# The last stage of an encoder block: h2 kept in the output tensor, half of the residual added by accumulating transfers, y handled in pairs of tiles

## The chip, the cores and the metric

One core of one Trainium2 chip runs the whole program. The metric is the device time of one launch in microseconds (us), the median of several runs. The profile is one execution taken by the hardware profiler. Its engines are PE (TensorE, matrix multiplication), DVE (VectorE), ACT (ScalarE), POOL (GpSimd) and SP (SyncE, which here only issues transfers). Each engine works through its own instructions in their fixed order and waits at an instruction until the data for it are there.

## What is computed

512 tokens of width 2048 pass through one layer: a mixing block with attention and a convolution, and then a gated feed-forward block. Only the end matters here:

```python
u = rms_norm(h, ffn_pre_g[l])            # h is called h2 below
gate, up = jnp.split(u @ w_gate_up[l], 2, axis=-1)
f = (jax.nn.silu(gate) * up) @ w_down[l] # f is called y below
h = h + rms_norm(f, ffn_post_g[l])
```

`rms_norm(x, g)` is x times 1/sqrt(mean(x*x) + 1e-6) times g, with the mean over the 2048 features of a token. So y must be complete for a token before its scale is known, and the residual h2 is added last.

## The kernel before

All activations are stored transposed: 128 features of a tile lie on the 128 partitions, and the tokens lie along the free dimension. y has 16 tiles of 128 features by 512 tokens. A is the first half of the tokens (256), B the second half.

h2 is made in the middle of the program (line 907): 16 stores of 128x512 put it into a scratch tensor in device memory, `h_d`. The product with `w_down` is cut along its 44 row tiles. Most of it is done earlier and summed up in a scratch tensor `y_d`. The last four row tiles (`DN_3`) are left for the end, which works so:

1. `half(0)` handles tokens A, `half(1)` tokens B. Each runs over 8 pairs of tiles, o = 0, 2, ..., 14. For a pair, `four` (line 1066) issues 24 matmuls of 128x256 into one PSUM bank, `pl`: 12 for each of the two tiles. Line 1199 adds the part of `y_d` to each tile, on DVE. Line 1202 squares each tile on ACT into `ysq`. Line 1210 sums the squares of the pairs on DVE. In the second half, line 1206 also writes y times the gain g into `yg`, on ACT.
2. The squares of the last two tiles are not added on DVE. Line 1212 folds the sum from 512 to 256 columns, and TensorE adds all of it over the partitions (line 357, `r_s`), three products of which the last waits for the last square.
3. `rstd` makes 1/rms: DVE scales and adds the epsilon (line 365, `r_v`), POOL raises it to the power -1/2 (line 367, `r_r`), and TensorE spreads the result over all partitions (line 374, `r_b`).
4. For tokens A, `finish` multiplies each of 16 tiles by g and `r_b` (line 1242, DVE), adds h2 (line 1248, three of four on POOL, one on DVE) and stores it (line 1249, SP's queue). h2 comes from `h_d` in the tiles `ha`. 12 of the 16 tiles are put between the work of the second half by a priority, and the last 4 are done after the last sum of squares.
5. For tokens B, `yg` is held in four groups of four tiles. After the last `r_b`, line 1260 multiplies each group by it. Group 0 is added into the output by an accumulating transfer, over a copy of h2 that was stored there before. For groups 1 to 3, line 1266 adds h2 from the tiles `hb` in two parts on DVE, and line 1271 stores each part, in turn on SP's and ACT's queues.

TensorE's order matters: `r_s` and `r_b` of tokens A (called `r40_s` and `r40_b`) stand among the matmuls of the second half, in the order that the program's scheduler gives, as far as the program does not pin it (`keep_in_program_order`).

Of the kernel before, what the change touches and what calls it, by code (L numbers as in the profile page):

```python
# [74 lines left out]
def hybrid_block(ctx: ExitStack, tc, xT, vecs, rpb, mask, w_c0, w_qk, w_v, w_gg, w_cg, w_ao, w_co, w_out, w_g0, w_gu, w_dn, outT):  # L75
# [1084 lines left out]
    for o in range(KT):  # L1160
        if o == KT - 2:
            added()
        tc.keep_in_program_order(nc.gpsimd.dma_start(y[o][:, A], y_d[0, o, :, A]))
    ha = []

    def second_loads(o):

        if o == KT - AHEAD:
            for i in range(KT):
                load_in_order(y[i][:, B], y_d[0, i, :, B])  # L1170
        elif o == KT - AHEAD + 2:
            for i in range(0, KT - 4, 4):
                t = stp.tile([P, 4, HN], F32, tag="S" if i else "S1", name=f"ha{i}")
                load_in_order(t, h_d[i : i + 4, :, A].rearrange("k p t -> p k t"))
                ha.extend(t[:, m] for m in range(4))
            for i in range(KT - 4, KT, 2):
                t = stp.tile([P, 2, HN], F32, tag="quad", name=f"ha{i}", bufs=3)
                load_in_order(t, h_d[i : i + 2, :, A].rearrange("k p t -> p k t"))
                ha.extend((t[:, 0], t[:, 1]))

    yg, r4 = [], []

    def half(n, between={}):

        cols, other = ((A, B), (B, A))[n]
        acc, last = None, []
        for o in range(0, KT, 2):
            if n == 0 and o + AHEAD < KT:
                kept(o + AHEAD)
# [6 lines left out]
            sq = [slot(f"ysq{n}_{o}")] * 2 if o < KT - 2 else [slot(f"ysq{n}_{o + i}") for i in range(2)]  # L1196
            for i, part in enumerate((other, cols)):
                t = y[o + i][:, cols]
                add = nc.vector.tensor_tensor(out=t, in0=ps[:, part], in1=t, op=ALU.add)
                if n == 0:  # L1200
                    tc.keep_in_program_order(add)
                nc.scalar.activation(sq[i][:, part if o < KT - 2 else cols], t, AF.Square)
                if n:
                    if (o + i) % 4 == 0:
                        yg.append(wp.tile([P, 4, HN], F32, tag="raw", name=f"yg{o}", bufs=5))
                    nc.scalar.activation(yg[-1][:, (o + i) % 4], t, AF.Copy, scale=col(C_FPOST, o + i))
            if o == 0:
                acc = sq[0]
            elif o < KT - 2:
                nc.vector.tensor_tensor(out=acc, in0=acc, in1=sq[0], op=ALU.add)  # L1210
# [14 lines left out]
    hb = []

    def first_half():
        s2()
        for i in range(0, KT, 4):
# [1 line left out]
            load_in_order(hb[-1], h_d[i : i + 4, :, B].rearrange("k p t -> p k t"))
        for g in range(G_ADD):

            nc.sync.dma_start(ov[4 * g : 4 * g + 4, :, B].rearrange("k p t -> p k t"), hb[g])
        with tc.high_priority(offset=-TAIL):
            finish(range(KT - LEFT), False)

    def finish(ms, pin):

        for m in ms:  # L1240
            ym = y[m][:, A]
            ins = nc.vector.scalar_tensor_tensor(  # L1242
                out=ym, in0=ym, scalar=col(C_FPOST, m), in1=r4[-1][:, A], op0=ALU.mult, op1=ALU.mult
            )
            if pin:
                tc.keep_in_program_order(ins)
            e = nc.vector if m % 4 == 3 else nc.gpsimd
            e.tensor_tensor(out=ym, in0=ym, in1=ha[m], op=ALU.add)  # L1248
            nc.sync.dma_start(ov[m, :, A], ym)
# [7 lines left out]
    for g, t in enumerate(yg):

        out = hb[g] if g < G_ADD else t
        tc.keep_in_program_order(nc.vector.tensor_tensor(out=out, in0=t, in1=rb, op=ALU.mult))  # L1260
        if g < G_ADD:
            nc.gpsimd.dma_start(ov[4 * g : 4 * g + 4, :, B].rearrange("k p t -> p k t"), out, accum_op=ALU.add)
            continue
        for m in range(0, 4, 2):
            tc.keep_in_program_order(
                nc.vector.tensor_tensor(  # L1266
                    out=t[:, m : m + 2], in0=t[:, m : m + 2], in1=hb[g][:, m : m + 2], op=ALU.add
                )
            )
            q = nc.scalar if m else nc.sync  # L1270
            q.dma_start(ov[4 * g + m : 4 * g + m + 2, :, B].rearrange("k p t -> p k t"), t[:, m : m + 2])
# [86 lines left out]
```

## Time and profile before

| what | us |
|---|---|
| median of 3 runs | 2492.33 (2490.29 to 2495.18) |
| span of the profiled execution, first to last instruction | 2489.2 |
| median less span | 3.1 |
| PE busy | 2464.8 (99%) |
| DVE busy | 2073.3 (83%) |
| ACT busy | 1246.1 (50%) |
| POOL busy | 493.3 (20%) |

The profiled execution has no time of its own in the profile apart from its span. A row of the timeline gives start, duration, engine, line, operation, output and inputs, shapes, and in brackets how long the engine had stood idle and what ended that. Start plus duration of one instruction can lie after the start of the next, since instructions of one engine overlap a little at their ends. SPq and ACTq are the queues that issue transfers.

### The profile page before, as it was taken

What the parts mean: (1) busy time and instruction counts of PE and PEld (TensorE: products, weight loads), DVE (VectorE), ACT (ScalarE), POOL (GpSimd) and SP (SyncE); (2) the same over time, 40 slices, a digit from 0 to 9 for tenths busy, and PEclk for the clock granted to TensorE, in tenths of its full rate; (3) what the DMA queues carried; (4) which work ended last, traced back from release to release, by engine and by line L of the source; (5) the groups of instructions that cost most, each with busy time, mean ns of one, the idle gap of its engine ahead of it and who ended that gap; (6) DMA issues with size and microseconds to landing.
All of it is one profiled execution on the core that took longest, in us unless ns stands there. A gap on an engine that the chain in (4) does not pass through costs nothing. (4 is left out here: it accounts for less than half of the span.)

```text
span 2489.2 us, 36170 instructions
## 1 busy us (share of the span) xinstructions
PE 2464.8 (99%) x13495; PEld 2141.7 (86%) x13495; DVE 2073.3 (83%) x2743; ACT 1246.1 (50%) x1939; POOL 493.3 (20%) x583
## 2 busy tenths in 40 slices
PE   9999999999999999999999999999999999999997
PEld 8888888888888888889998888888888888888887
DVE  5999887497777668878898888889898889989887
ACT  5223333355555434556455555555555565456553
POOL 0110242220000000021111111122222203632352
PEclk9999999999999999999999999999999999999998
DMA  6246222376667544669456655666666678888986
GB/s 215 89 144 207 101 103 101 135 253 196 190 187 228 184 142 136 205 215 301 138 166 178 185 170 171 184 195 213 205 200 195 220 234 238 237 230 255 226 222 195
DMA packets 165104, 472.37 MB, mean 190 GB/s; under 512 B 18752, under 2 KB 30656, under 8 KB 164928
## 3 DMA queue, kind: packets, MB, share of 16 engines
q1 hardware_dynamic: 109584, 334.02, 39.1%
q0 software_dynamic: 32928, 97.54, 18.4%
q10 hardware_dynamic: 22416, 38.50, 4.1%
q8 instruction: 106, 1.74, 0.3%
q14 instruction: 70, 0.57, 0.1%
HBM read 396.06 MB, written 71.30 MB: 188 GB/s over the span
## 5 line engine op out<-in xcount | busy, mean ns | idle before, releaser
L450 DVE SCALAR_TENSOR_TENSOR cv<-z,vec,cv 128x497 f32<-128x497 f32 (+14 forms) x240 | 188.4, 786 | 4.8
L971 POOL TENSOR_TENSOR row<-row,asq 128x512 f32<-128x512 f32 x30 | 54.6, 1821 | 402.8 <-ACT asq L970 402.8
L1126 POOL TENSOR_TENSOR ys<-ys,row 128x512 f32<-128x512 f32 x32 | 57.6, 1801 | 119.8 <-DVE ys L347 100.1
L146 ACT CAST whi_qk<-raw_qk 128x1024 fp32r<-128x1024 f32 x32 | 33.7, 1053 | 79.2 <-PE qk L196 58.2
L147 DVE TENSOR_TENSOR wlo_qk<-raw_qk,whi_qk 128x1024 fp32r<-128x1024 f32 x32 | 40.4, 1262 | 37.9 <-ACT whi_qk L146 37.8
L993 POOL TENSOR_TENSOR an<-an,row 128x512 f32<-128x512 f32 x32 | 55.3, 1729 | 72.1 <-DMA an<-a_d 45.7
L146 ACT CAST whi_y<-raw_y 128x1024 fp32r<-128x1024 f32 x31 | 32.6, 1051 | 64.9 <-PE py L196 52.7
L760 DVE TENSOR_TENSOR gg<-py,gg 128x512 f32<-128x512 f32 x32 | 21.9, 687 | 46.4 <-PE py L197 43.4
L531 POOL TENSOR_TENSOR bm<-braw,msk 128x64 f32<-128x64 f32 x96 | 54.3, 600 | 14.8 <-DMA braw<-in_rpb 14.7
L193 PE MATMUL py<-ycl,whi_y 128*128 128x512 f32 x128 | 49.9, 390 | 0.0
L196 PE MATMUL py<-ych,whi_y 128*128 128x512 f32 x128 | 49.8, 389 | 0.0
L197 PE MATMUL py<-ych,wlo_y 128*128 128x512 f32 x128 | 49.8, 389 | 0.0
L147 DVE TENSOR_TENSOR wlo_y<-raw_y,whi_y 128x1024 fp32r<-128x1024 f32 x31 | 37.8, 1224 | 9.0 <-ACT whi_y L146 8.6
L458 POOL TENSOR_TENSOR csum<-csum,cv 128x512 f32<-128x512 f32 x7 | 12.7, 1816 | 141.4 <-DVE cv L450 141.4
L177 PE MATMUL f<-b,wlo_f 128*128 128x256 f32 x128 | 36.3, 283 | 0.0
L176 PE MATMUL f<-b,whi_f 128*128 128x256 f32 x128 | 36.3, 283 | 0.0
L175 PE MATMUL f<-b,whi_f 128*128 128x256 f32 x128 | 36.3, 283 | 0.0
L146 ACT CAST whi_ca<-raw_ca 128x1024 fp32r<-128x1024 f32 x12 | 12.6, 1054 | 46.3 <-PE cb L196 18.1
L787 POOL DMA_DIRECT2D m_d<-m x8 | 4.4, 555 | 136.9 <-ACT m L169 75.0
L568 ACT ACTIVATE sc<-sc,st 128x256 f32<-128x256 f32 x32 | 16.1, 504 | 30.8 <-DVE st L567 30.8
L1127 POOL DMA_DIRECT2D y_d<-ys x32 | 29.4, 918 | 9.4 <-POOL ys L1126 7.8
L1056 DVE TENSOR_TENSOR sg<-sg,su 128x512 f32<-128x512 f32 x39 | 30.0, 770 | 0.0
(3251 smaller groups left out, 8755.6 us busy)
## 6 DMA issues: line engine op xcount, KB each, us to landing
raw_qk<-in_w_qk SPq DMA_DIRECT2D x32, 512.0 KB, 3.3
raw_w<-in_w_dn SPq DMA_DIRECT2D x24, 512.0 KB, 5.4
a_d<-sg ACTq DMA_DIRECT2D x44, 256.0 KB, 4.0
raw_v<-in_w_v SPq DMA_DIRECT2D x16, 512.0 KB, 4.3
gg<-g_d SPq DMA_DIRECT2D x32, 256.0 KB, 4.1
raw_y<-in_w_co SPq DMA_DIRECT2D x16, 512.0 KB, 3.6
raw_f<-in_w_g SPq DMA_DIRECT2D x16, 512.0 KB, 3.9
an<-a_d POOLq DMA_DIRECT2D x32, 256.0 KB, 5.5
```

What stands on the lines that cost most here:

```text
L146: cast(hi[:, s], raw[:, s])
L147: nc.vector.tensor_tensor(out=lo[:, s], in0=raw[:, s], in1=hi[:, s].bitcast(F32), op=ALU.subtract)
L175: nc.tensor.matmul(o, hi, t[:, B], start=first, stop=False, skip_group_check=True)
L176: nc.tensor.matmul(o, hi, t[:, A], start=False, stop=False, skip_group_check=True)
L193: mmul = nc.tensor.matmul(ps, hi[:, s], al, start=first, stop=False)
L196: nc.tensor.matmul(ps, hi[:, s], ah, start=False, stop=False)
L197: nc.tensor.matmul(ps, lo[:, s], ah, start=False, stop=last)
L450: nc.vector.scalar_tensor_tensor(out=a[:, to], in0=z[:, fr], scalar=col(C_WDW, i * CW + w), in1=a[:, to], op0=ALU.mult, op1=ALU.add)
L531: nc.gpsimd.tensor_tensor(out=bm[:, o + i - i0], in0=raw[:, :, min(max(i, 0), 3) * EC : (min(max(i, 0), 3) + 1) * EC], in1=msk[:, o + i - ...
L971: nc.gpsimd.tensor_tensor(out=row[n], in0=row[n], in1=sq, op=ALU.add)
L993: ins = nc.gpsimd.dma_start(t, a_d[DN_P + k]), nc.gpsimd.tensor_tensor(out=t, in0=t, in1=row[k // KT], op=ALU.mult)
L1126: tc.keep_in_program_order(nc.gpsimd.tensor_tensor(out=t, in0=t, in1=row[n], op=ALU.mult))
```

## The change

- `h_d` is gone. h2 is stored into the output tensor instead, with the same 16 stores on ACT's queue.
- y is held in tiles of a pair for one half of the tokens (128x2x256), so each pair is loaded by one transfer instead of two, and the add and the square of a pair are one instruction of 128x512 each. The last pair still has two of each.
- The gain g is now multiplied in on ACT in both halves, in place for tokens A.
- 1/rms is made by a square root on ACT (with 1/2048 and the epsilon in the same instruction) and a reciprocal on DVE.
- Tokens A: DVE multiplies a pair by `r_b` (8 instructions of 128x512), and an accumulating transfer on POOL's queue adds it into the output, where h2 already lies. The loads `ha`, the 16 adds and the 16 stores are gone, and so is the priority: the 8 multiplications stand where the program writes them.
- Tokens B: group 0 is added by an accumulating transfer as before, now without a copy of h2 first. The four multiplications come first, then the adds: the first parts of groups 1 and 2 on POOL, the other four parts on DVE.

The core of the diff:

```diff
-                nc.scalar.dma_start(h_d[i], f[i])
+                nc.scalar.dma_start(ov[i], f[i])
...
+    def weighted(n, o):
+        t = y[n][o // 2][:, o % 2]
+        return nc.scalar.activation(yg[-1][:, o % 4] if n else t, t, AF.Copy, scale=col(C_FPOST, o))
...
-            for i, part in enumerate((other, cols)):
-                t = y[o + i][:, cols]
-                add = nc.vector.tensor_tensor(out=t, in0=ps[:, part], in1=t, op=ALU.add)
-                nc.scalar.activation(sq[i][:, part if o < KT - 2 else cols], t, AF.Square)
+            if o < KT - 2:
+                tc.keep_in_program_order(nc.vector.tensor_tensor(out=t, in0=halves, in1=t, op=ALU.add))
+                sq = slot(f"ysq{n}_{o}")
+                nc.scalar.activation(sq.rearrange("p (m t) -> p m t", m=2), t, AF.Square)
+                if o:
+                    nc.vector.tensor_tensor(out=acc, in0=acc, in1=sq, op=ALU.add)
...
-            lambda: r.append(rstd(squares, D, f"r4{n}", blocks, pin)),
+            nc.scalar.activation(r, ps[:, : NB // 2], AF.Sqrt, bias=eps, scale=1.0 / D)
+            nc.vector.reciprocal(r, r)
...
-        with tc.high_priority(offset=-TAIL):
-            finish(range(KT - LEFT), False)
+        ra = r4[0][:, None].broadcast_to([P, 2, HN])
+        for o in range(0, KT, 2):
+            t = y[0][o // 2]
+            nc.vector.tensor_tensor(out=t, in0=t, in1=ra, op=ALU.mult)
+            nc.gpsimd.dma_start(ov[o : o + 2, :, A].rearrange("k p t -> p k t"), t, accum_op=ALU.add)
...
-    finish(range(KT - LEFT, KT), True)
+    tc.keep_in_program_order(weighted(1, KT - 1))
     last2()
...
+    scale_group(0)
+    tc.keep_in_program_order(
+        nc.gpsimd.dma_start(ov[:4, :, B].rearrange("k p t -> p k t"), yg[0], accum_op=ALU.add)
+    )
+    scale_group(1)
+    add_part(nc.gpsimd, nc.sync, 1, 0)
+    scale_group(2)
+    add_part(nc.gpsimd, nc.sync, 2, 0)
+    scale_group(3)
+    for n, (g, m) in enumerate(((1, 2), (2, 2), (3, 0), (3, 2))):
+        add_part(nc.vector, (nc.scalar, nc.sync)[n % 2], g, m)
```

The new order follows from the code and from the scheduler, which places again what is not pinned. Three places matter. Names carry the half and the pair: `pl1_12` is the PSUM bank of pair 12 in the second half (tokens B), `y4b` is pair 4 of tokens B, `r40` belongs to tokens A and `r41` to tokens B. The line numbers after the change are not those of before.

TensorE, where the 1/rms of tokens A is spread, before:

```order
L1066 MATMUL pl1_4_23586<-fa43h_23105,wl5h_23135 128x256
L1066 MATMUL pl1_4_23586<-fa43h_23105,wl5l_23136 128x256
L374 MATMUL r40_b_23611<-ident_77,r40_r_23576 128x128 x2
L1066 MATMUL pl1_6_23668<-fa40l_23094,wl6h_23187 128x256
L1066 MATMUL pl1_6_23668<-fa40h_23093,wl6h_23187 128x256
```

The same place of TensorE after the change:

```order
L1063 MATMUL pl1_12_23709<-fa43l_23105,wl13h_23306 128x256
L1063 MATMUL pl1_12_23709<-fa43h_23104,wl13h_23306 128x256
L1063 MATMUL pl1_12_23709<-fa43h_23104,wl13l_23307 128x256
L372 MATMUL r40_b_23583<-ident_77,r40_23486 128x128 x2
L1063 MATMUL pl1_6_23615<-fa40l_23093,wl6h_23180 128x256
L1063 MATMUL pl1_6_23615<-fa40h_23092,wl6h_23180 128x256
```

Before, `r40_b` stood behind the pairs 0, 2 and 4 of the second half. Now it stands behind the pairs 0, 2, 4, 8 and 12, and the pairs 6, 10 and 14 come after it.

DVE in the second half, before:

```order
L1199 TENSOR_TENSOR y4_23153<-pl1_4_23586,y4_23153 128x256
L1199 TENSOR_TENSOR y5_23154<-pl1_4_23586,y5_23154 128x256
L1242 SCALAR_TENSOR_TENSOR y0_23149<-y0_23149,vec_75,r40_b_23611 128x256
L1242 SCALAR_TENSOR_TENSOR y1_23150<-y1_23150,vec_75,r40_b_23611 128x256
L1210 TENSOR_TENSOR ysq1_0_23534<-ysq1_0_23534,ysq1_4_23659 128x512
L1242 SCALAR_TENSOR_TENSOR y2_23151<-y2_23151,vec_75,r40_b_23611 128x256
L1242 SCALAR_TENSOR_TENSOR y3_23152<-y3_23152,vec_75,r40_b_23611 128x256
L1242 SCALAR_TENSOR_TENSOR y4_23153<-y4_23153,vec_75,r40_b_23611 128x256
L1199 TENSOR_TENSOR y6_23155<-pl1_6_23668,y6_23155 128x256
```

DVE at that place after the change:

```order
L1194 TENSOR_TENSOR y2b_23157<-pl1_2_23518,y2b_23157 128x512
L1253 TENSOR_TENSOR y0a_23148<-y0a_23148,r40_b_23583 128x512
L1253 TENSOR_TENSOR y2a_23149<-y2a_23149,r40_b_23583 128x512
L1198 TENSOR_TENSOR ysq1_0_23514<-ysq1_0_23514,ysq1_2_23553 128x512
L1253 TENSOR_TENSOR y4a_23150<-y4a_23150,r40_b_23583 128x512
L1253 TENSOR_TENSOR y6a_23151<-y6a_23151,r40_b_23583 128x512
L1253 TENSOR_TENSOR y8a_23152<-y8a_23152,r40_b_23583 128x512
L1253 TENSOR_TENSOR y10a_23153<-y10a_23153,r40_b_23583 128x512
L1253 TENSOR_TENSOR y12a_23154<-y12a_23154,r40_b_23583 128x512
L1253 TENSOR_TENSOR y14a_23155<-y14a_23155,r40_b_23583 128x512
L1194 TENSOR_TENSOR y4b_23158<-pl1_4_23558,y4b_23158 128x512
L1198 TENSOR_TENSOR ysq1_0_23514<-ysq1_0_23514,ysq1_4_23610 128x512
```

Before, the multiplications of tokens A were spread between the adds of tokens B. Now all eight stand in one block ahead of the add of pair 4, and the add and the sum of squares of the pairs 4, 6, 8, 10 and 12 follow one after the other.

DVE at the end, before (the first row is the last of the adds of y):

```order
L1199 TENSOR_TENSOR y15_23164<-pl1_14_23803,y15_23164 128x256
L365 TENSOR_SCALAR r41_v_23843<-r41_s_23836 128x2
L1242 SCALAR_TENSOR_TENSOR y12_23161<-y12_23161,vec_75,r40_b_23611 128x256
L1242 SCALAR_TENSOR_TENSOR y13_23162<-y13_23162,vec_75,r40_b_23611 128x256
L1242 SCALAR_TENSOR_TENSOR y14_23163<-y14_23163,vec_75,r40_b_23611 128x256
L1242 SCALAR_TENSOR_TENSOR y15_23164<-y15_23164,vec_75,r40_b_23611 128x256
L1248 TENSOR_TENSOR y15_23164<-y15_23164,ha14_23444 128x256
L1260 TENSOR_TENSOR hb0_23614<-yg0_23537,r41_b_23859 128x1024
L1260 TENSOR_TENSOR yg4_23662<-yg4_23662,r41_b_23859 128x1024
L1266 TENSOR_TENSOR yg4_23662<-yg4_23662,hb4_23616 128x512 x2
```

DVE at the end after the change:

```order
L1205 TENSOR_TENSOR y14b_23163<-pl1_14_23742,y14b_23163 128x256 x2
L1238 RECIPROCAL r41_23774<-r41_23774 128x2
L1264 TENSOR_TENSOR yg0_23512<-yg0_23512,r41_b_23785 128x1024
L1264 TENSOR_TENSOR yg4_23608<-yg4_23608,r41_b_23785 128x1024
L1264 TENSOR_TENSOR yg8_23671<-yg8_23671,r41_b_23785 128x1024
L1264 TENSOR_TENSOR yg12_23734<-yg12_23734,r41_b_23785 128x1024
L1268 TENSOR_TENSOR yg4_23608<-yg4_23608,hb4_23586 128x512
L1268 TENSOR_TENSOR yg8_23671<-yg8_23671,hb8_23588 128x512
L1268 TENSOR_TENSOR yg12_23734<-yg12_23734,hb12_23590 128x512 x2
```

The four multiplications and the add that belong to tokens A have left the end. Of the six adds of tokens B, four are left on DVE, behind all multiplications.

More of the change, by code (lines that the diff above doesn't have):

```diff
@@ L66 @@
 AHEAD = 6
-LEFT, G_ADD = 4, 1
 RE_EARLY = 11
@@ L1156, in hybrid_block, with load_y @@
     pairs(1, *products_and_operands(1, DN_2), DN_3)
-    y = [slot(f"y{o}") for o in range(KT)]
-    for o in range(KT):
+    y = [[slot(f"y{o}{n}", shape=(P, 2, HN)) for o in range(0, KT, 2)] for n in "ab"]
+    def load_y(q, n, o):
+        ins = q.dma_start(y[n][o // 2], y_d[0, o : o + 2, :, (A, B)[n]].rearrange("k p t -> p k t"))
+        tc.keep_in_program_order(ins)
+    for o in range(0, KT, 2):
         if o == KT - 2:
             added()
[L1163 to L1181, printed above, removed]
+        load_y(nc.gpsimd, 0, o)
+    yg = []
+    def weighted(n, o):
+        t = y[n][o // 2][:, o % 2]
+        return nc.scalar.activation(yg[-1][:, o % 4] if n else t, t, AF.Copy, scale=col(C_FPOST, o))
     def half(n, between={}):
-        cols, other = ((A, B), (B, A))[n]
-        acc, last = None, []
+        cols = (A, B)[n]
+        acc = None
         for o in range(0, KT, 2):
@@ L1189, in half @@
                 kept(o + AHEAD)
-            elif n == 0:
-                second_loads(o)
+            elif n == 0 and o == KT - AHEAD:
+                for i in range(0, KT, 2):
+                    load_y(nc.sync, 1, i)
             ps = (bank, abank)[o // 2 % 2](f"pl{n}_{o}")
-            for i, part in enumerate((other, cols)):
+            for i, part in enumerate((A, B)):
                 four(ps[:, part], *w[o + i], cols)
             between.get(o, lambda: None)()
-            sq = [slot(f"ysq{n}_{o}")] * 2 if o < KT - 2 else [slot(f"ysq{n}_{o + i}") for i in range(2)]
@@ L1197, in half @@
-            for i, part in enumerate((other, cols)):
-                t = y[o + i][:, cols]
[L1199 to L1210, printed above, removed]
-            if o == KT - 4:
-                nc.vector.tensor_tensor(out=acc[:, cols], in0=acc[:, cols], in1=acc[:, other], op=ALU.add)
-        return acc, *sq
-    def halved(n, squares, pin=False):
-        r = []
-        blocks = range(n * NB // 2, (n + 1) * NB // 2)
-        return (
-            lambda: r.append(rstd(squares, D, f"r4{n}", blocks, pin)),
-            lambda: r4.insert(0, by_column(r[0], f"r4{n}", blocks, pin)),
-        )
+            t = y[n][o // 2]
@@ new lines, in half @@
+            halves = ps.rearrange("p (m t) -> p m t", m=2)
+            if n and o % 4 == 0:
+                yg.append(wp.tile([P, 4, HN], F32, tag="raw", name=f"yg{o}", bufs=5))
+            if o < KT - 2:
[4 more added lines that the diff above has]
+                    nc.vector.tensor_tensor(out=acc, in0=acc, in1=sq, op=ALU.add)
+                else:
+                    acc = sq
+            else:
+                last = []
+                for i in range(2):
+                    tc.keep_in_program_order(
+                        nc.vector.tensor_tensor(out=t[:, i], in0=halves[:, i], in1=t[:, i], op=ALU.add)
+                    )
+                    last.append(slot(f"ysq{n}_{o + i}"))
+                    nc.scalar.activation(last[i][:, A], t[:, i], AF.Square)
@@ new lines, in half, with sums @@
+            if o == KT - 4:
+                tc.keep_in_program_order(
+                    nc.vector.tensor_tensor(out=acc[:, A], in0=acc[:, A], in1=acc[:, B], op=ALU.add)
+                )
+            for i in range(2 - (n and o == KT - 2)):
+                ins = weighted(n, o + i)
+                if o == KT - 2:
+                    tc.keep_in_program_order(ins)
+        return acc, *last
+    eps = const.tile([P, 1], F32, name="eps")
+    nc.gpsimd.memset(eps, EPS)
+    r4 = []
+    def halved(n, squares, pin=False):
+        r = const.tile([P, NB // 2], F32, name=f"r4{n}")
+        def sums():
+            ps = abank(f"r4{n}_s")
+            for i, a in enumerate(squares):
+                for t in range(NB // 2):
+                    mmul = nc.tensor.matmul(
+                        ps[:, t : t + 1], a[:, t * P : (t + 1) * P], ones[:, 0:1],
+                        start=i == t == 0, stop=i == len(squares) - 1, skip_group_check=True,
+                    )
+                    if pin:
+                        tc.keep_in_program_order(mmul)
+            nc.scalar.activation(r, ps[:, : NB // 2], AF.Sqrt, bias=eps, scale=1.0 / D)
+            nc.vector.reciprocal(r, r)
+        return sums, lambda: r4.append(by_column(r, f"r4{n}", range(NB // 2), pin)[:, A])
@@ L1224, in hybrid_block @@
     s1, s2 = halved(0, half(0), pin=True)
[L1225 removed]
+    hb = [None]
     def first_half():
         s2()
[L1229 removed]
+        for i in range(4, KT, 4):
             hb.append(wp.tile([P, 4, HN], F32, tag=("whi", "wlo")[i // 4 % 2], name=f"hb{i}"))
[L1231 to L1236 removed]
@@ L1238, in finish @@
[L1238 to L1249, printed above, removed]
+            load_in_order(hb[-1], ov[i : i + 4, :, B].rearrange("k p t -> p k t"))
@@ L1257, in hybrid_block @@
[L1257 to L1271, printed above, removed]
+    rb = r4[1][:, None].broadcast_to([P, 4, HN])
```

12 lines of the change are left out of this document (9 added, 3 removed).

## The prediction

> **What bounds the kernel now.** I read the page first: engine shares, then the 40 slices.
>
> ```profile
> span 2489.2 us, 36170 instructions
> PE 2464.8 (99%) x13495; PEld 2141.7 (86%) x13495; DVE 2073.3 (83%) x2743; ACT 1246.1 (50%) x1939; POOL 493.3 (20%) x583
> ```
>
> TensorE is busy to the end, and the change leaves its 13,000 matmuls as they are. So only the end, where TensorE runs out of work, can give or take time. The table of windows shows where that is:
>
> ```profile
> 2460.00:2470.00 10.00, 10.00 (x86) 10.00 (x84) 8.92 (x20) 5.49 (x15) 4.10 (x5) 1.00 0.40 133
> 2470.00:2480.00 10.00, 3.25 (x18) 2.50 (x17) 8.32 (x15) 1.66 (x5) 4.32 (x5) 0.71 0.18 62
> ```
>
> The columns are PE, PEld, DVE, ACT and POOL. DVE is busy 8.92 and 8.32 of 10 us there. The chain of waits and the timeline give the steps:
>
> ```profile
> 2469.94 0.28 PE L1066 MATMUL pl<-fa43h,wl15l 128*128 128x256 f32 x1
> 2470.84 0.75 DVE L1199 TENSOR_TENSOR y<-pl,y 128x256 f32<-128x256 f32 x2
> 2472.07 0.40 ACT L1202 ACTIVATE ysq<-y 128x256 f32<-128x256 f32 x1
> 2472.52 0.62 PE r_s L357 x4
> 2473.17 0.16 DVE L365 TENSOR_SCALAR r_v<-r_s 128x2 f32<-128x2 f32 x1 [1.58 <-PE r_s L357]
> 2473.41 0.71 POOL L367 TENSOR_TENSOR r_r<-r_v,mhalf 128x2 f32<-128x2 f32 x1 [6.04 <-DVE r_v L365]
> 2474.17 1.22 PE L374 MATMUL r_b<-ident,r_r 128*128 128x128 f32 x4 [1.04 <-POOL r_r L367]
> 2475.70 1.21 DVE L1260 TENSOR_TENSOR hb<-yg,r_b 128x1024 f32<-128x1024 f32 x1
> 2482.99 1.29 DVE L1266 TENSOR_TENSOR yg<-yg,hb 128x512 f32<-128x512 f32 x2
> 2484.36 0.38 ACTq L1271 DMA_DIRECT2D out<-yg  x1
> ```
>
> So I cut the end in two at 2475.70, where DVE starts on tokens B's output. Ahead of it runs the chain: last matmul, last adds, last square, `r_s`, 1/rms, `r_b`. Behind it lie 13.5 us (2489.2 less 2475.70): DVE's multiplications and adds until 2484.28 (8.6 us), then 4.9 us for the last store.
>
> **The start of the last stretch.** If DVE had nothing else, the change would bring it forward. The four multiplications of tokens A (1.66 us in the chain) and their add stand no longer ahead, the fold no longer delays the last adds, and POOL's 0.71 us is replaced. For the new steps the nearest rows are these:
>
> ```profile
> 1.19 1.28 ACT L119 ACT_TABLE_LOAD   x1 [1.19 <-PEq L1345]
> 2.48 0.20 ACT L119 ACTIVATE mhalf<-ones 128x4 f32<-128x4 f32 x1
> L569 DVE RECIPROCAL st<-st x32: 142/157/166, 299.1 to 485.2; 128x1 f32<-128x1 f32 x32
> ```
>
> The square root of 128x2 costs about 0.20, the reciprocal 0.16, with hand-overs of 0.04 each 0.5 us in all, against 1.0 us from `r_s` to `r_b` before (2473.17 to 2474.17). Table loads stand once in ACT's new order, ahead of the first square root, where ACT waits for `r_s` anyway: nothing if hidden, 1.28 us if not.
>
> But the order of the instructions says that DVE will have something else. `r_b` of tokens A now comes two pairs later on TensorE. The pace:
>
> ```profile
> 2445.25 0.28 PE L1066 MATMUL pl<-fa40l,wl0h 128*128 128x256 f32 x1
> 2451.01 1.40 PE L357 MATMUL r_s<-ones,ysq 128*128 128x1 f32 x12
> 2455.22 0.60 PE L374 MATMUL r_b<-ident,r_r 128*128 128x128 f32 x4
> ```
>
> Two pairs take 2451.01 less 2445.25, so 5.76 us or 2.88 a pair. `r_b` moves from 2455.22 to about 2460.98, and its result is there at 2461.6. In front of DVE's block stands the first multiplication, so DVE waits there with the adds of pairs 4, 8 and 12 behind it, though TensorE has finished those pairs. Behind this wait come 8 multiplications and one sum, then pair after pair an add, a square on ACT, and a sum that waits for the square. This alternation can be measured in the first half of before, where the same three steps followed each other:
>
> ```profile
> 2440.37 0.75 DVE L1199 TENSOR_TENSOR y<-pl,y 128x256 f32<-128x256 f32 x2
> 2440.82 0.75 ACT L1202 ACTIVATE ysq<-y 128x256 f32<-128x256 f32 x2 [1.47 <-DVE y L1199]
> 2441.60 0.69 DVE L1210 TENSOR_TENSOR ysq<-ysq,ysq 128x512 f32<-128x512 f32 x1 [0.48 <-ACT ysq L1202]
> 2442.21 0.75 DVE L1199 TENSOR_TENSOR y<-pl,y 128x256 f32<-128x256 f32 x2
> 2412.60 0.69 DVE L328 TENSOR_TENSOR d<-d,d_14v 128x512 f32<-128x512 f32 x1
> L970 ACT ACTIVATE asq<-sg 128x512 f32<-128x512 f32 x30 | 19.0, 633 | 5.5 <-issue 4.5 <-DVE sg L1056 0.9
> ```
>
> One round took 1.84 us. With pairs as one instruction it is 0.69 (add from PSUM) + 0.03 + 0.63 (square) + 0.04 + 0.61 (from the sum's start to the next instruction) = 2.0 us, since a square can no longer start when the first tile of a pair is ready. The sum:
>
> - 2461.65: first multiplication; 9 instructions of 128x512 at 0.61 end at 2467.1.
> - Five rounds of 2.0 us (pairs 4 to 12): 2477.1. TensorE has been done since 2470.
> - Fold 0.45, two adds 0.76, last square 0.45: 2478.8. `r_s` 0.62 and hand-overs: 2479.45.
> - Square root and reciprocal 0.45, `r_b` 1.22 and hand-overs: 2481.2.
>
> Against 2475.70 that is 5.5 us later. The uncertain pieces are the round (1.84 to 2.1 over five rounds: -0.8 to +0.5) and the first half. There ACT gets two more instructions a pair (0.49 each):
>
> ```profile
> 2427.85 0.74 DVE L1199 TENSOR_TENSOR y<-pl,y 128x256 f32<-128x256 f32 x2
> 2433.92 0.75 DVE L1199 TENSOR_TENSOR y<-pl,y 128x256 f32<-128x256 f32 x2
> 2437.14 0.75 DVE L1199 TENSOR_TENSOR y<-pl,y 128x256 f32<-128x256 f32 x2
> L1206 ACT ACTIVATE yg<-y,vec 128x256 f32<-128x256 f32 x16 | 7.9, 495 | 3.6 <-DVE y L1199 3.6
> ```
>
> The casts of the weights for pairs 8 to 14 go through that queue. A round of 3.2 us there becomes about 3.8. From the first add at 2427.85 on, the weights of pair 14 are then ready at 2443.2, and TensorE, which now has 13 matmuls of the second half mixed in, wants the last of them at about 2444.7. I take nothing; if the cover fails, up to 1 us.
>
> **The last stretch.** Before, DVE had four multiplications (1.13 to 1.21) and six adds (0.61 to 0.69) in it: 8.6 us. Now it has the four (4.6 us) and four adds (2.5 us): 7.1 us if nothing blocks it. What can block it is POOL, which adds two parts beside it:
>
> ```profile
> 2423.43 1.41 POOL L1126 TENSOR_TENSOR ys<-ys,row 128x512 f32<-128x512 f32 x1 [0.19 <-DVE ys L347]
> 2424.04 1.34 DVE L156 TENSOR_TENSOR wl6l<-raw_w,wl6h 128x512 fp32r<-128x512 f32 x1
> 2425.31 2.62 DVE L156 TENSOR_TENSOR wl7l<-raw_w,wl7h 128x512 fp32r<-128x512 f32 x1
> 2425.75 1.63 POOL L1126 TENSOR_TENSOR ys<-ys,row 128x512 f32<-128x512 f32 x1
> 2478.42 1.37 POOL L1262 DMA_DIRECT2D out<-hb  x1 [2.06 <-DVE yg L1260]
> ```
>
> A DVE instruction that took 0.69 elsewhere took 1.34 and 2.62 beside a POOL add, and ended 0.5 us after it. POOL starts on group 0's transfer 2.7 us after DVE's first multiplication began and issues for 1.37, so its two adds (1.3 to 1.8 each) run from about 4.0 to 6.7 us. DVE comes to its adds at 4.6: the first waits until about 5.3, the second until about 6.7, and the fourth ends at 8.6. The gain of 1.5 us is then gone. The Trainium skill, SBUF — State Buffer, Who interferes with whom, says the same as a rule: a VectorE instruction with two SBUF inputs and a GpSimd instruction that reads SBUF exclude each other for the whole instruction. By it the stretch keeps its 8.6 us; by the undisturbed rows it would be 7.1.
>
> Behind the last add come the stores. The traffic stays: one accumulating transfer of 512 KB and six stores of 256 KB.
>
> ```profile
> out<-hb POOLq DMA_DIRECT2D x1, 512.0 KB, 7.0
> 2484.00:2485.00 1.00, 0.00 (x0) 0.00 (x0) 0.28 (x1) 0.00 (x0) 0.00 (x0) 0.50 1.21 245
> 2486.00:2487.00 1.00, 0.00 (x0) 0.00 (x0) 0.00 (x0) 0.00 (x0) 0.00 (x0) 0.50 1.09 384
> ```
>
> The transfers ran at 245 GB/s beside the accumulating one and at 384 without it, at a full share of the DMA engines. In the new order the stores start some 2 us later and closer together, so they catch up no time: 0 to 0.6 us more than 4.9. I take +0.3 and for the whole last stretch 0.0, with -1.5 to +0.8.
>
> **Other edits.** h2's 16 stores have the same size and queue; the loads, adds and stores of tokens A that go away were off the chain apart from the last four tiles, counted above. Eight accumulating transfers of 256 KB now run from about 2463. Group 0's 512 KB took 7.0 us to land, so 2 MB strictly one behind the other take up to 28 us (2491). In the last 15 us of the span its queue showed this:
>
> ```profile
> q0 software_dynamic: 528, 0.52, 25.0%
> ```
>
> 25% of 15 us are 3.75 us of all DMA engines for 0.52 MB, so 15 us for 2 MB if they overlap well. I take the shorter, done near 2479, ahead of group 0's transfer (about 2484); the longer is a rival.
>
> **The sum.** +5.5 and 0.0, on a span of 2489.2. The median lies 3.1 us above this span; I keep that: 2492.3 + 5.5 = 2497.8 us, slower by 0.22%. Its own range, from the bounds (-0.8 to +1.5 ahead, -1.5 to +0.8 behind), is 2495.5 to 2500.
>
> **Rivals.** A difference under 0.2% (5 us) can't be told from none here, so small terms decide the sign.
>
> - The last stretch keeps its gain (27%). The start is late as above, but POOL's adds are over before DVE comes to its own, or slip behind them, and the stretch takes 1.5 us less: 2496.3, within 0.2%. For it speaks that POOL's spans are rough; against it the rows of 1.34 and 2.62 us.
> - Accumulating transfers collide (10%). If the eight of tokens A are still under way at 2484, group 0's waits for them and lands 2 to 4 us later: about 2500.5. It decides from 21 us for the eight on. Against it: DMA was at 0.40 of its share at 2460 to 2470.
> - Faster (8%): the queue on DVE clears in time. If `r_b` of tokens A reached DVE by 2456, as before, or the rounds overlapped so that the add of pair 12 started when TensorE was done with it, the last adds would start at 2470.3, and the chain of 3.5 us would bring the last stretch to 2473.9: 1.8 us earlier, with 0 to 1.5 behind, about 2489.5. The point is the block's end: it must lie 10 us ahead of 2467, and by the order it lies at 2467.1. Against it stands an order that the chip can't change.
>
> **How the numbers follow.** The forecast's own case has 55%. It lies only 0.5 us above the bound, so I count 8 of these 55 as the same. Slower: 47 + 10 = 57%; same: 27 + 8 = 35%; faster 8%. The range leaves out most of the faster case and the far end of the collisions, and allows 1.5 us for the medians beyond the two ends: 2494.0 to 2500.5.
>
> **What would show it.** Right: in the new trace DVE stands idle for 2 us or more ahead of the first multiplication of tokens A, until `r_b` at about 2461; the rounds of pairs 4 to 12 follow at 2.0 us; the last `r_s` comes near 2479 though TensorE's last matmul of `pl` ends near 2470. In the last stretch the first two adds of DVE last over 1 us. Wrong: the first multiplication of group 0 starts before 2479, or the accumulating transfers of tokens A land behind 2484.

## The result and the profile after

The changed kernel took 2498.5 us (median of 7 runs, 2496.14 to 2499.24) against 2491.39 us for the kernel before (7 runs, 2490.03 to 2495.18): a ratio of 1.0026, with a 95% interval of 1.0016 to 1.0035. It is slower, inside the forecast range. The profiled execution has a span of 2496.7 us, 7.5 more than the one before. The page of the changed kernel says where those 7.5 us are not:

```profile
PE 2465.6 (99%) x13495; PEld 2141.9 (86%) x13495; DVE 2064.9 (83%) x2715; ACT 1253.3 (50%) x1944; POOL 489.6 (20%) x572
```

TensorE has its 13495 matmuls and 0.8 us more of busy time (2465.6 against 2464.8): the new time is time in which TensorE waits. The timeline of TensorE and DVE, from DVE's reciprocal for 1/rms of tokens A on:

```profile
2459.91 0.17 DVE L1238 RECIPROCAL r<-r 128x2 f32<-128x2 f32 x1 [7.32 <-ACT r L1237]
...
2462.63 0.60 PE L372 MATMUL r_b<-ident,r 128*128 128x128 f32 x4
...
2463.27 0.69 DVE L1253 TENSOR_TENSOR y0a<-y0a,r_b 128x512 f32<-128x512 f32 x1 [2.59 <-PE r_b L372]
...
2468.67 0.68 DVE L1194 TENSOR_TENSOR y4b<-pl,y4b 128x512 f32<-128x512 f32 x1
...
2470.05 0.69 DVE L1198 TENSOR_TENSOR ysq<-ysq,ysq 128x512 f32<-128x512 f32 x1 [0.70 <-ACT ysq L1196]
...
2470.65 0.69 DVE L1194 TENSOR_TENSOR y6b<-pl,y6b 128x512 f32<-128x512 f32 x1
...
2471.59 0.28 PE L1063 MATMUL pl<-fa43h,wl15l 128*128 128x256 f32 x1
...
2476.62 0.69 DVE L1194 TENSOR_TENSOR y12b<-pl,y12b 128x512 f32<-128x512 f32 x1
...
2478.73 0.43 DVE L1211 TENSOR_TENSOR ysq<-ysq 128x256 f32<-128x256 f32 x1
2479.07 0.75 DVE L1205 TENSOR_TENSOR y14b<-pl,y14b 128x256 f32<-128x256 f32 x2
2479.30 2.69 PE L1231 MATMUL r_s<-ones,ysq 128*128 128x1 f32 x12 [7.43 <-DVE ysq L1211]
...
2479.52 0.74 ACT L1208 ACTIVATE ysq<-y14b 128x256 f32<-128x256 f32 x2 [0.75 <-DVE y14b L1205]
...
2482.63 1.19 PE L372 MATMUL r_b<-ident,r 128*128 128x128 f32 x4 [0.64 <-DVE r L1238]
2483.86 4.61 DVE L1264 TENSOR_TENSOR yg<-yg,r_b 128x1024 f32<-128x1024 f32 x4 [1.38 <-PE r_b L372]
```

The bracket behind `y0a` is the wait that was forecast: DVE idles 2.59 us for `r_b` of tokens A. The bracket behind the reciprocal is a second wait, which the prediction does not name: `r_s` of tokens A has moved on TensorE as well. Its last product ends at 2459.57, 12.02 us ahead of the last matmul's start, where it ended 17.53 ahead in before. The reciprocal that needs it stands ahead of the add of pair 2 in DVE's order, so DVE idles 7.32 us there. Of the 5.76 us by which `r_b` comes later, 5.51 are thus already in `r_s`. Then the block of eight multiplications and one sum takes until 2468.67. From there the adds of pairs 4 to 12 come every 1.99 us (2468.67, 2470.65, ... 2476.62), each sum waiting 0.70 us for the square on ACT. The last matmul starts at 2471.59, and the last two adds only at 2479.07: TensorE idles 7.43 us ahead of `r_s`.

One row was not forecast, the last `r_s`. The last square ends at 2479.52 + 0.74 = 2480.26, `r_s` at 2479.30 + 2.69 = 2481.99. That is 1.73 us where before took 0.67 (2472.47 to 2473.14, of which the chain shows 0.62). Two windows of the changed kernel give the clock (the third column from the right is the mean granted clock):

```profile
2474.00:2475.00 1.00, 0.00 (x0) 0.00 (x0) 0.98 (x2) 0.79 (x2) 1.00 (x2) 0.76 1.19 181
...
2481.00:2482.00 1.00, 0.99 (x5) 0.91 (x5) 0.00 (x0) 0.00 (x0) 0.00 (x0) 0.50 0.00 0
```

After the last matmul of `pl` TensorE has nothing to do, and from about 2474.5 on its granted clock is 0.50 (a mean of 0.76 in the window where it changes). Before, `r_s` ran in 2471 to 2473, at 1.00.

To compare executions I cut the end at two points that every one of them has: M, the start of the last matmul of `pl`, and T, the start of DVE's first multiplication of group 0 (2475.70 in before).

| kernel | M | T - M | end - T | M to the end |
|---|---|---|---|---|
| before | 2469.94 | 5.76 | 13.50 | 19.26 |
| changed | 2471.59 | 12.27 | 12.84 | 25.11 |
| e1_pin | 2468.74 | 5.66 | 12.60 | 18.26 |
| e2_spread | 2470.10 | 3.66 | 12.74 | 16.40 |
| e3_spread_only | 2469.14 | 8.99 | 12.77 | 21.76 |
| e4_dve_adds | 2468.39 | 12.28 | 12.83 | 25.11 |
| e5_busy | 2469.52 | 11.33 | 12.65 | 23.98 |
| e6_singles | 2469.31 | 13.34 | 12.55 | 25.89 |
| e7_no_acc0 | 2468.68 | 12.28 | 11.44 | 23.72 |
| e8_again (changed, once more) | 2469.47 | 12.29 | 12.74 | 25.03 |

From M on, the changed kernel takes 25.11 - 19.26 = 5.85 us more: 6.51 up to T, less 0.66 behind it. The other 1.65 us of the 7.5 lie ahead of M. Each row is one profiled execution; T - M lies between 12.27 and 12.29 in the four that share everything up to T (changed, e4, e7 and e8).

### The profile page after: what moved, and what is told of

Its sections match the earlier page's. It is cut to its first block, busy times and chain, and to the rows that moved or that the text cites. A ratio compares the mean times of both kernels' runs of the same rounds, so it can differ in the third digit from the quotient of the medians.

```text
span 2496.7 us, 36069 instructions
## 1 busy us (share of the span) xinstructions
PE 2465.6 (99%) x13495; PEld 2141.9 (86%) x13495; DVE 2064.9 (83%) x2715; ACT 1253.3 (50%) x1944; POOL 489.6 (20%) x572
```

## The experiments

### Is the time ahead of M part of the change?

The kernel of e8 is the changed kernel, unaltered.

> The changed kernel itself once more. In its first profile the last matmul of the end started 1.65 us later than in the kernel before, and the end from there took 5.85 us longer; only the second belongs to the change by the queue theory, since TensorE's work up to there is the same. Scatter theory: the start of the last matmul falls near 2469 as in the five experiments that share this part (2468.4 to 2469.5), the end from there is 25.1 us again, and the time is 5 to 6 us above the kernel before, ratio 1.0020 to 1.0024. Rival (the change also costs time ahead of the end): the last matmul starts 1.5 us or more later than in the kernel before again, and the ratio is 1.0028 or more.

```profile
2469.47 0.28 PE L1063 MATMUL pl<-fa43h,wl15l 128*128 128x256 f32 x1
...
2481.76 4.62 DVE L1264 TENSOR_TENSOR yg<-yg,r_b 128x1024 f32<-128x1024 f32 x4 [1.38 <-PE r_b L372]
```

Measured: 2495.91 us (11 runs) against 2490.61 us (15 runs), ratio 1.0021 (1.0012 to 1.0030). M lies at 2469.47, 0.47 ahead of that of before, and the end from M is 25.03. The expectation of the scatter theory held in all its numbers. In the kernels that share TensorE's order (all but before, e1 and e2) M runs from 2468.39 to 2469.52, and only the first profile of the changed kernel has it later, at 2471.59. The 11 runs of e8 alone spread over 2.5 us, more than the 1.65. The change costs 5.3 us by this comparison and 5.8 us by the end from M alone.

### Where TensorE gives 1/rms of tokens A

```diff
-                four(ps[:, part], *w[o + i], cols)
+                four(ps[:, part], *w[o + i], cols, pin=n == 1)
```

> The matmuls of the second half stand in the order of the program, so that r_b of tokens A comes behind pair 4 again and not behind pair 12; all else is as in the changed kernel. Queue theory (DVE was held at the first multiplication of tokens A until r_b came, and the rounds behind it ended late): r_b comes about 5.8 us sooner, DVE no longer idles 2.6 us there, the block of 8 multiplications ends near 2463 instead of 2468.7, the rounds of 2.0 us keep the pace of TensorE, and DVE starts on group 0 5 to 6 us sooner than 2483.9: time near 2492.5 us, about that of the kernel before (within 1.5 us). The first half may lose up to 1 us to weights that come late, since the second half's matmuls no longer fill in there. Rival (the transfers that add tokens A, or the longer rounds themselves, make the end late): the start on group 0 stays within 1 us of 2483.9 and the time near 2498.5.

TensorE's last matmul, and DVE at the places shown above, now in e1:

```profile
2453.35 0.17 DVE L1238 RECIPROCAL r<-r 128x2 f32<-128x2 f32 x1 [3.62 <-ACT r L1237]
...
2454.67 0.69 DVE L1253 TENSOR_TENSOR y0a<-y0a,r_b 128x512 f32<-128x512 f32 x1 [0.54 <-PE r_b L372]
...
2460.06 0.68 DVE L1194 TENSOR_TENSOR y4b<-pl,y4b 128x512 f32<-128x512 f32 x1
...
2468.02 0.68 DVE L1194 TENSOR_TENSOR y12b<-pl,y12b 128x512 f32<-128x512 f32 x1
...
2468.74 0.28 PE L1063 MATMUL pl<-fa43h,wl15l 128*128 128x256 f32 x1
...
2474.40 4.61 DVE L1264 TENSOR_TENSOR yg<-yg,r_b 128x1024 f32<-128x1024 f32 x4 [1.38 <-PE r_b L372]
```

Measured: 2489.13 us (11 runs) against 2490.41 us for before (21 runs), ratio 0.9996 (0.9987 to 1.0005). This one edit takes the whole loss away: T lies 5.66 us behind M (5.76 in before). DVE's wait for `r_b` is 0.54 us instead of 2.59, its wait ahead of the reciprocal 3.62 instead of 7.32, together 5.75 less, and the block ends at 2460.06. The edit brings back both places: `r_s` of tokens A ends 17.53 us ahead of M again, and `r_b` starts 14.72 ahead, each as in before. So e1 shows TensorE's order as the cause, not the place of `r_b` alone. With only `r_b` moved, at most 2.55 us could have been had (an estimate from rows of the changed kernel: the reciprocal ends at 2460.08, `r_b` starts at 2462.63); no run moved it alone. The median came 3.4 us lower than expected, mostly because I had started from the first profile of the changed kernel, whose M lay 2.85 us later. The rounds still set the pace behind the block: from the add of pair 4 to that of pair 12 there are four of 1.99 us, and the last sum of squares comes behind TensorE's last matmul.

### The block of eight multiplications

```diff
+    def scale_a(o):
+        t = y[0][o // 2]
+        ra = r4[0][:, None].broadcast_to([P, 2, HN])
+        tc.keep_in_program_order(nc.vector.tensor_tensor(out=t, in0=t, in1=ra, op=ALU.mult))
+        nc.gpsimd.dma_start(ov[o : o + 2, :, A].rearrange("k p t -> p k t"), t, accum_op=ALU.add)
...
-                four(ps[:, part], *w[o + i], cols)
+                four(ps[:, part], *w[o + i], cols, pin=n == 1)
...
+                for m in range(2 * o - 8, 2 * o - 4, 2) if n and 4 <= o < KT - 4 else ():
+                    scale_a(m)
...
-        for o in range(0, KT, 2):
-            t = y[0][o // 2]
-            nc.vector.tensor_tensor(out=t, in0=t, in1=ra, op=ALU.mult)
-            nc.gpsimd.dma_start(ov[o : o + 2, :, A].rearrange("k p t -> p k t"), t, accum_op=ALU.add)
```

> As the first experiment, and the eight multiplications of tokens A stand two by two between the add and the sum of squares of pairs 4, 6, 8 and 10, where DVE would otherwise wait for the square. Queue theory: a round is then 0.69 + 2 x 0.61 + 0.61 = 2.5 us for four pairs, under TensorE's 2.88 a pair, so DVE is there when TensorE ends: last adds about 1 us behind the last matmul, r_s 2 us and the start on group 0 5.5 us behind it, 2476 to 2477 by the profile of the changed kernel, 7 us sooner: near 2491 us, and 0 to 2 us less than the first experiment. Rival (the rounds are bound by the square on ACT and not by the queue on DVE): no difference from the first experiment. Rival (transfers): near 2498.5 again.

The same places in e2:

```profile
2464.66 0.69 DVE L1201 TENSOR_TENSOR y10b<-pl,y10b 128x512 f32<-128x512 f32 x1 [0.40 <-PE pl L1063]
...
2467.54 0.69 DVE L1201 TENSOR_TENSOR y12b<-pl,y12b 128x512 f32<-128x512 f32 x1 [0.40 <-PE pl L1063]
...
2470.10 0.28 PE L1063 MATMUL pl<-fa43h,wl15l 128*128 128x256 f32 x1
...
2470.42 0.76 DVE L1214 TENSOR_TENSOR y14b<-pl,y14b 128x256 f32<-128x256 f32 x2 [0.33 <-PE pl L1063]
...
2473.04 0.68 PE L372 MATMUL r_b<-ident,r 128*128 128x128 f32 x4 [0.65 <-DVE r L1247]
...
2473.76 4.61 DVE L1268 TENSOR_TENSOR yg<-yg,r_b 128x1024 f32<-128x1024 f32 x4 [0.87 <-PE r_b L372]
```

Measured: 2487.46 us (11 runs), ratio to before 0.9989 (0.9980 to 0.9997): faster than both kernels, and 1.7 us less than e1 on the same chip. The brackets of the adds of pairs 10 and 12 now name TensorE: DVE waits for matmuls and not the other way round. The last adds start 0.32 us behind the start of the last matmul, T is 3.66 us behind M, and `r_b` takes 0.68 us instead of 1.19, since TensorE's clock is still at 1.00 there (window 2473 to 2474). T was expected 5.5 us behind M and the time near 2491: T came 1.8 us sooner and the time 3.5 us lower than that. `r_s` ended 2.3 us behind M, and from there to T it took 1.36 us, where the expectation allowed 3.5.

The third kernel has only the second edit of these two: the multiplications are spread, but `four` is not pinned, so `r_s` and `r_b` of tokens A stay where the changed kernel has them.

> The eight multiplications of tokens A stand two by two behind the adds of pairs 4, 6, 8 and 10, as in the second experiment, but TensorE's order is that of the changed kernel, with r_b of tokens A behind pair 12. It divides the 8.6 us between the changed kernel and the second experiment (12.3 against 3.7 us from the start of the last matmul to the start on group 0). Queue theory: DVE waits for r_b behind the add of pair 4 instead of ahead of it, then two multiplications and a sum (1.8 us), three rounds of 2.4 to 2.5, one of 2.0: the last add of pair 12 starts about 10 us behind r_b, and the start on group 0 comes 6.5 to 7.5 us behind the last matmul, so about 5 us sooner than in the changed kernel and 3 us later than in the second experiment; near 2492.5 us. Rival (the late r_b alone is the cause, the block costs nothing): 12 us behind the last matmul, as in the changed kernel. Rival (the block alone is the cause): 3.7 us, as in the second experiment.

```profile
2460.82 0.69 DVE L1179 TENSOR_TENSOR y0a<-y0a,r_b 128x512 f32<-128x512 f32 x1 [0.54 <-PE r_b L372]
...
2470.89 0.68 DVE L1201 TENSOR_TENSOR y12b<-pl,y12b 128x512 f32<-128x512 f32 x1
...
2473.57 2.69 PE L1240 MATMUL r_s<-ones,ysq 128*128 128x1 f32 x12 [4.15 <-DVE ysq L1220]
```

Measured: 2492.61 us (10 runs) against 2490.34 us (13 runs), ratio 1.0009 (1.0000 to 1.0019), T - M 8.99. Both parts count. TensorE's order, with `r_s` and `r_b` late, costs 5.3 us with spread multiplications (8.99 - 3.66) and 6.6 with the block (12.27 - 5.66); the block costs 2.0 with them early (5.66 - 3.66) and 3.3 with them late (12.27 - 8.99). DVE waits only 0.54 us for `r_b` itself here, but 7.31 ahead of the reciprocal (3.63 in e2): the late order delays the multiplications by both. T - M was expected at 6.5 to 7.5. The add of pair 12 starts 10.1 us behind the end of `r_b` (2460.18 + 0.60), as expected; the difference lies behind it. `r_s` ended 1.72 us behind the last square instead of 0.67, and `r_b` took 1.19 us instead of the 0.68 of e2, once more after an idle TensorE (the bracket, 4.15 us).

### The clock ahead of the last sum

```diff
+FILL = 56
...
+    def keep_busy():
+        pw = bank("busy")
+        for _ in range(FILL):
+            tc.keep_in_program_order(
+                nc.tensor.matmul(pw[:, A], w[0][0][:, :P], acts[0][0][:, A], start=True, stop=True, skip_group_check=True)
+            )
-    last1, last2 = halved(1, half(1, {2: s1, 4: first_half}))
+    last1, last2 = halved(1, half(1, {2: s1, 4: first_half, 14: keep_busy}))
```

> 56 matmuls of 128x256 whose result nobody uses stand on TensorE behind its last pair, so that it does not idle for the 7 us ahead of r_s; all else is as in the changed kernel. Clock theory (r_s ended 1.7 us behind the last square instead of 0.6 because TensorE had idled and was granted half the clock): the granted clock stays near 1.0 until r_s, r_s ends 0.6 to 0.8 us behind the last square and r_b takes 0.6 instead of 1.2, so the start on group 0 comes 1.0 to 1.7 us sooner relative to the last square. Rival (r_s is late for another reason, its wait or its first products): r_s ends 1.7 us behind the last square whatever the clock.

The last sum in e5, with the square that it waits for and the square root behind it:

```profile
2477.23 1.74 PE L1232 MATMUL r_s<-ones,ysq 128*128 128x1 f32 x12 [0.72 <-DVE ysq L1212]
2477.45 0.75 ACT L1209 ACTIVATE ysq<-y14b 128x256 f32<-128x256 f32 x2 [0.75 <-DVE y14b L1206]
...
2479.62 1.20 PE L373 MATMUL r_b<-ident,r 128*128 128x128 f32 x4 [0.65 <-DVE r L1239]
```

One profiled execution, no interval. The last square ends at 2478.20 and `r_s` at 2478.97, so 0.77 us against 1.73, and T - M is 11.33 against 12.27: 0.94 us sooner. That part of the clock theory holds. The other part fell: `r_b` still took 1.20 us. The fillers end at 2476.5, and the windows of e5 show the clock down again by `r_b`, although `r_s` ran in between:

```profile
2478.00:2479.00 1.00, 0.98 (x8) 0.89 (x8) 0.00 (x0) 0.60 (x2) 0.00 (x0) 1.00 0.00 0
...
2480.00:2481.00 1.00, 0.82 (x4) 0.52 (x3) 0.15 (x1) 0.00 (x0) 0.00 (x0) 0.50 0.00 0
```

### One instruction for a pair, or two

```diff
-                tc.keep_in_program_order(nc.vector.tensor_tensor(out=t, in0=halves, in1=t, op=ALU.add))
                 sq = slot(f"ysq{n}_{o}")
-                nc.scalar.activation(sq.rearrange("p (m t) -> p m t", m=2), t, AF.Square)
+                for i in range(2) if n else (slice(0, 2),):
+                    tc.keep_in_program_order(
+                        nc.vector.tensor_tensor(out=t[:, i], in0=halves[:, i], in1=t[:, i], op=ALU.add)
+                    )
+                    nc.scalar.activation(sq.rearrange("p (m t) -> p m t", m=2)[:, i], t[:, i], AF.Square)
```

> In the second half the add and the square of a pair are two instructions of 128x256 each again, as before the change; all else is as in the changed kernel. Step of the prediction (a round of 2.0 us with one instruction a pair, 1.84 with two): the five rounds behind the block of multiplications take 9.2 us instead of 10.0 and the start on group 0 comes 11.5 us behind the last matmul instead of 12.3. Rival (other limits set the round, such as the two products with the gain that share ACT): no shorter round.

One round in e6, on DVE and on ACT:

```profile
2466.39 0.75 DVE L1197 TENSOR_TENSOR y4b<-pl,y4b 128x256 f32<-128x256 f32 x2
...
2466.84 0.42 ACT L1199 ACTIVATE ysq<-y4b 128x256 f32<-128x256 f32 x1 [7.14 <-DVE y4b L1197]
...
2467.16 0.49 ACT L1173 ACTIVATE yg<-y4b,vec 128x256 f32<-128x256 f32 x1
...
2467.56 0.40 ACT L1199 ACTIVATE ysq<-y4b 128x256 f32<-128x256 f32 x1
...
2468.61 0.75 DVE L1197 TENSOR_TENSOR y6b<-pl,y6b 128x256 f32<-128x256 f32 x2
```

One profiled execution. The round is 2.22 us (2466.39 to 2468.61), longer than the 1.99 of the pairs, and T - M grows by 1.07. The expectation fell, and so did what it was drawn from: in the first half of before, where 1.84 us were read, no product with the gain ran on ACT. Here a product of 0.49 stands between the two squares. One instruction for a pair saved about 1.1 us in this place (five rounds of 0.22).

### The last stretch

Two kernels ask what the work behind T is bound by. In e4 GpSimd's two adds go back to DVE:

```diff
-    add_part(nc.gpsimd, nc.sync, 1, 0)
+    add_part(nc.vector, nc.sync, 1, 0)
     scale_group(2)
-    add_part(nc.gpsimd, nc.sync, 2, 0)
+    add_part(nc.vector, nc.sync, 2, 0)
```

> The two adds that GpSimd does in the last stretch go back to DVE; all else is as in the changed kernel. Theory that GpSimd's adds block DVE's (8.6 us forecast with them, 7.1 without any disturbance): DVE's adds of 128x512 go from 0.7 to 1.3 us each back to 0.61, six of them, and the stretch from DVE's first multiplication to its last add is 4.6 + 6 x 0.61 = 8.3 us against 7.96 in the changed kernel, so the change gained at most 0.3 us of the 1.2 that taking two adds away promises. Rival (no blocking; GpSimd's adds are free): the same 8.3 us, but the rows of DVE's adds are as long with GpSimd's adds beside them as without.

In e7 the transfer of group 0 is left out:

```diff
-    tc.keep_in_program_order(
-        nc.gpsimd.dma_start(ov[:4, :, B].rearrange("k p t -> p k t"), yg[0], accum_op=ALU.add)
-    )
```

> The accumulating transfer of group 0 at the end is left out, so that the output lacks y in those four tiles; all else is as in the changed kernel. It asks what sets the end of the last stretch (12.84 us from DVE's first multiplication of group 0, of which DVE's last add ends at 7.96). Transfer theory (moving all bytes of the last stretch takes the same time, so DVE's shorter work is given back): with 512 KB less the stretch ends 1 us or more sooner, near 11.5 us. Rival (the stretch is set by DVE's last add and the fixed time of one store behind it): 12.8 us, unchanged, or 0.3 us less since GpSimd comes to its adds sooner.

First the changed kernel: POOL's two adds, DVE's first add by itself (a window that holds only this one), and all four.

```profile
2485.62 1.31 POOL L1273 DMA_DIRECT2D out<-yg  x1 [10.19 <-issue]
2486.44 3.01 POOL L1268 TENSOR_TENSOR yg<-yg,hb 128x512 f32<-128x512 f32 x2
```

```profile
2488.40 1.61 DVE L1268 TENSOR_TENSOR yg<-yg,hb 128x512 f32<-128x512 f32 x1
```

```profile
2488.40 3.42 DVE L1268 TENSOR_TENSOR yg<-yg,hb 128x512 f32<-128x512 f32 x4
```

Then DVE's adds in e4 (with no add on POOL), and POOL's and DVE's in e7:

```profile
2483.06 0.69 DVE L1268 TENSOR_TENSOR yg<-yg,hb 128x512 f32<-128x512 f32 x1
...
2486.66 2.49 DVE L1268 TENSOR_TENSOR yg<-yg,hb 128x512 f32<-128x512 f32 x4
```

```profile
2483.45 2.49 POOL L1268 TENSOR_TENSOR yg<-yg,hb 128x512 f32<-128x512 f32 x2 [10.92 <-issue]
2485.49 2.81 DVE L1268 TENSOR_TENSOR yg<-yg,hb 128x512 f32<-128x512 f32 x4
```

GpSimd's adds do hold DVE up: its first add took 1.61 us beside them and ended at 2490.01, after POOL (2486.44 + 3.01 = 2489.45); in e4, without them, an add took 0.69. The four multiplications beside POOL were not lengthened: the four take 4.61 us, and in e4, with no add on POOL, two take 2.35 and a single one 1.21, which is the same step of 1.13 to 1.14 from one to the next. The Trainium skill, SBUF — State Buffer, Who interferes with whom, states both halves: a VectorE instruction with two SBUF inputs contends with a GpSimd instruction that reads SBUF, and one with at most one SBUF input, outside its two-port modes (which this kind of instruction lacks, by the same section), does not. The adds here read two SBUF tiles, and the multiplications read `r_b` from PSUM, where TensorE wrote it. The trace agrees in both halves: 1.61 us against 0.69 for the add, 1.13 to 1.14 either way for the multiplication.

But DVE's time alone does not set the end. In e4 DVE is done 8.48 us behind T (2486.66 + 2.49 - 2480.67) instead of 7.96 (8.3 expected, so the change gained 0.5 us there and not 0.3), and the end is the same, 12.83 against 12.84. In e7 it comes 1.40 us sooner, at 11.44, near the 11.5 of the transfer theory. DVE's last add ends 0.62 sooner (7.34 behind T), since POOL's two adds take 2.49 us instead of 3.01 with no transfer issued beside them, and the span ends 4.10 us behind that add instead of 4.88. So the transfers take part in setting the end, by 0.8 us at least; how the other 0.6 divides was not separated. The DMA queues of the changed kernel in the window from 2484 to 2497 show how dear the accumulating transfer is (columns: packets, MB, share of all DMA engines in the window):

```profile
q0 software_dynamic: 528, 0.52, 30.2%
q1 hardware_dynamic: 1088, 1.05, 23.0%
```

0.52 MB added by the accumulating transfer took 30.2% of the window, twice as many bytes stored plainly on SP's queue 23.0%: 2.65 times the DMA time per byte.

## Why the prediction was right, step by step

- **`r_b` of tokens A two pairs later: right.** Forecast 5.76 us later on TensorE. It lies 8.96 us ahead of M (2471.59 - 2462.63) where it lay 14.72 ahead (2469.94 - 2455.22): 5.76 later. e1 shows that TensorE's order is the cause: with `r_s` and `r_b` back in their old places, T - M returns to 5.66. What the prediction left out is that `r_s` moved too, by 5.51 us. DVE therefore idles 9.91 us in two waits (7.32 ahead of the reciprocal, 2.59 ahead of the block) against 4.16 in e1. The sum did not suffer, since it starts from `r_b`.
- **The block, 5.45 us: right.** 2463.27 to 2468.67 are 5.40.
- **Five rounds of 2.0 us: right in size, wrong in part of the reason.** 2468.67 to the fold at 2478.73 are 10.06 us. But the pair in one instruction shortened the round, from 2.22 to 1.99 (e6); the 1.84 us taken for the old way belonged to a place without the products on ACT.
- **Fold, adds, last square: right.** Forecast 1.7, measured 1.53 (2478.73 to 2480.26).
- **`r_s` 0.62 us behind the last square: wrong, the term of the sum that failed.** It took 1.73. The row of 0.62 (0.67 with the hand-over) was measured on a TensorE that had just been at work, while the same prediction said that TensorE would stand idle from 2470 on. I took `r_b` at 1.22 us, which was already the price at half clock, and did not ask the same of `r_s`. With TensorE kept busy it took 0.77 (e5). That is the 1.0 us between T as forecast (5.5 later) and as measured (6.51).
- **Square root, reciprocal, `r_b`: right.** 0.64 us from `r_s` to `r_b` instead of 1.04; the table load (1.28 us, at 2454.63 on ACT) lies ahead of `r_s` of tokens A, for which ACT then still waits 3.70 us.
- **The last stretch at 0.0 with -1.5 to +0.8: off by 0.66, on the side of the rival.** I had the first two adds of DVE blocked, until 6.7 us behind T. POOL's adds ran from 2.58 to 5.59 us: POOL began to issue the transfer 1.76 us behind T and not 2.7, and went on to its adds 0.8 us later. So one add was blocked and not two: the mechanism was right, the time at which POOL starts was off. The end came 0.66 sooner than in before, but not by DVE alone: e4 gives back 0.5 of DVE's gain and ends at the same time.
- **First half, nothing: right.** The adds of y there come every 3.82 us, as forecast, and the window up to 2470 shows no idle TensorE:

```profile
2437.17 0.68 DVE L1194 TENSOR_TENSOR y4a<-pl,y4a 128x512 f32<-128x512 f32 x1
...
2440.99 0.68 DVE L1194 TENSOR_TENSOR y6a<-pl,y6a 128x512 f32<-128x512 f32 x1
```

```profile
2430.00:2470.00 40.00, 40.00 (x337) 40.00 (x336) 21.76 (x37) 20.98 (x43) 5.37 (x9) 1.00 0.43 113
```

- **Accumulating transfers of tokens A: right, the collision did not happen.** The last was issued at 2470.71 and landed 10.1 us later (the last column of the list of transfers), at 2480.8, ahead of group 0's at 2485.62:

```profile
2470.71 4.72 POOL L1254 DMA_DIRECT2D out<-y14a  x1
```

```profile
q0 software_dynamic: 2176, 2.10, 78.6%
...
out<-y14a POOLq DMA_DIRECT2D x1, 256.0 KB, 10.1
```

- **The faster rival.** It said that 1.8 us would be won up to T if DVE's queue cleared in time, and that the block would have to end 10 us sooner. e1 clears the block 5.8 us sooner relative to M (8.68 ahead of it, against 2.92 ahead) and wins 0.1 over before. e2 frees the adds from the block altogether: 2.1 us up to T and 0.8 behind it, 2.9 in all, and the medians differ by 2.95. The size was right; the order of the changed kernel excludes it.

So the sum of +5.5 stood against 5.8 by the trace and 5.3 to 7.1 by the medians; two errors of 1.0 and 0.7 with opposite signs nearly cancelled, which is luck. Of the first comparison's 7.1 us some 1.3 lie ahead of M; its interval (4.0 to 8.7 us) holds 5.8 as well, and e8 did not show them again.

That the time itself came out 0.7 us from the forecast (2498.5 against 2497.8) is partly luck too. The 3.1 us that the forecast adds to the span are no fixed cost: they evidently set the median of three runs against the span of another execution. Where a run's own time and span are both known they differ by 1.7 to 2.2 us, and by 1.8 in the profiled run of the changed kernel. This term was 1.3 too large, and M came 1.65 later than in before.

## What to carry to other kernels

Where a scheduler moves a small sum and the spread of its result on TensorE behind two more groups of matmuls, look at who waits for them in order: here a reciprocal and then eight multiplications on DVE, each behind a wait, held up the adds of pairs that TensorE had finished, and TensorE stood idle for 7.4 us ahead of the last sum. Put such work into the gaps where the waiting engine would idle anyway (between an add and a sum that needs another engine's square): the same instructions went from 6.5 us of loss up to T to 3.2 us of loss when they were spread, and to 2.1 us of gain when TensorE's order was pinned as well. And take the price of a small matmul from a row in the same state of the clock that the new order will leave.
